# The rows of the transposed tokens at sixteen different offsets modulo 512 bytes

## The chip, the cores and the metric

The kernel runs on one core of a Trainium2 chip. Five engines work side by side on a shared on-chip memory of 128 partitions: TensorE (PE, with its weight loads shown apart as PEld), VectorE (DVE), ScalarE (ACT), GpSimd (POOL) and SyncE (SP), which here only starts transfers. The metric is the device time of one execution in microseconds.

## What is computed

One block of a streaming encoder over 512 tokens of width 1024, in float32. The tokens are normalised and multiplied by one wide matrix, and the ten slices of the result feed two branches, stick-breaking attention with 8 heads and retention with 4 heads, which are gated, projected, merged and added to the input:

```python
h = rms_norm(x, norm_gain)
proj = einsum('bsd,dc->bsc', h, w_in)            # 1024 -> 10 x 1024
(sb_q, sb_k, sb_v, sb_g, r_q, r_k, r_v, r_g, m_sb, m_ret) = split(proj)
out_a = stick_breaking_attention(rms_norm(sb_q), rms_norm(sb_k), sb_v) * silu(sb_g)
out_b = rms_norm(chunkwise_retention(rotary(r_q), rotary(r_k), r_v)) * silu(r_g)
p_a, p_b = out_a @ w_branch_sb, out_b @ w_branch_ret
merged = sigmoid(m_sb + b0) * p_a + sigmoid(m_ret + b1) * p_b
x = x + merged @ w_out
```

## The kernel before

**Split products.** Every float32 operand of a large product is held as two tiles of the matmul's reduced type, a rounded part (`hi`) and the remainder (`lo`). A product is three matmuls, hi by hi, hi by lo and lo by hi (`mm3`, lines 91 to 95; line 86 issues every matmul). In the profile a matmul's row reads `out<-moving,stationary`: the first name behind the arrow is the operand that streams through the array, the second the one that was loaded as weights. Each matmul has a weight load of its own (PEld), which is made while the matmul ahead of it streams.

**The transposed tokens.** `xT_hi` and `xT_lo` (lines 142 and 143) hold the 512 tokens with the model's width on the partitions: 8 rows (`NK`) of 512 numbers, or 2,048 bytes, one row for each 128 of the 1,024 inputs. ACT (line 159) and DVE (line 160) write each row once at the start. Every later group of the input projection reads all 16 rows.

**Groups.** `dense` makes one group: for each of the 8 rows `k`, `load_split` brings 128 by 512 weights, splits them into `hi` and `lo` (lines 115 and 116, or 204 and 205), and for each of 4 blocks `j` one `mm3` adds into a PSUM bank. That is 8 x 4 x 3 = 96 matmuls of 128 x 512. Twenty groups are of the input projection and use `xT`: four each of `qk` and `rqk`, two each of `v`, `sg`, `rv`, `rg`, `ma` and `mb`, in all 1,920 matmuls. In the `qk`, `v` and `rv` groups (argument `rows` true) a 128-column slice of an `xT` row is the stationary operand and the weights stream; in the others the weights are stationary and a whole `xT` row streams. Six more groups (`pa`, `pb`, `fin`) have other tiles in the place of `xT`.

**Side work.** The small matmuls of attention (`z`, `pw`, `po`) and retention (`rz`, `ro`, `rt`) are generators that `Interleaver.step` puts between the matmuls of a group, after every second `j`. TensorE keeps the order of the program.

**Addresses.** The pool `const` lays its tiles one behind another in the order of the code, each rounded up to 32 bytes; the other pools follow. Two tiles have spare room: `vec` (`V_ROOM`) and `m_half` (`M_ROOM`). In the built program `xT_hi` starts at byte 17,888 of each partition and `xT_lo` at 34,272, both 480 modulo 512. A row is 2,048 bytes, so all 16 rows lie at 480. The weight tiles, the tiles of `qk`, `rqk`, `v` and `rv`, the gates, the branch outputs and the temporaries are at 480 as well, and a slice of 128 numbers is 512 bytes, so slices keep it. The one large exception is the pair `wT`, at 128: it streams in `po` and is stationary in `ro`.

Of the kernel before, what the change touches and what calls it, by code (L numbers as in the profile page):

```python
# [7 lines left out]
F32 = mybir.dt.float32  # L8
F32R = mybir.dt.float32r
# [3 lines left out]
P = 128  # L13
S = 512
D = 1024
NT = S // P
NK = D // P
# [9 lines left out]

V_NG, V_BM, V_QG, V_KG, V_RG, V_N = 0, 8, 24, 25, 26, 34

V_ROOM, M_ROOM = 66, 112  # L30


RAW_BUFS = 2
# [34 lines left out]
def hybrid_block(ctx, tc, x, x_t, vecs, w_in, w_a, w_b, w_o, cos_t, sin_t, decay, out):  # L68
# [3 lines left out]
    const = ctx.enter_context(tc.tile_pool(name="const", bufs=1))  # L72
# [66 lines left out]
    nc.scalar.activation(warm, zero, AF.Sigmoid)  # L139

    vec = const.tile([P, V_ROOM], F32, name="vec")[:, :V_N]
    xT_hi = const.tile([P, NK, S], F32R, name="xT_hi")
    xT_lo = const.tile([P, NK, S], F32R, name="xT_lo")

    def first_loads():

# [503 lines left out]
```

## Time and profile before

| | us |
|---|---|
| median of 2 runs | 663.17 |
| lowest, highest | 662.77, 663.58 |
| the profiled execution's own time | 664.18 |
| its span, first to last instruction | 662.4 |
| PE busy in it | 656.3 |
| PEld busy | 546.4 |
| DVE, ACT, POOL busy | 375.9, 260.7, 50.8 |

The span and all rows are of one profiled execution; 1.8 us of its time lie outside the span. Matmuls are pipelined: the start of the next one is earlier than the modelled end of the one before, so the distance of the starts, not the duration, is what a matmul takes from the span.

### The profile page before, as it was taken

What the parts mean: (1) busy time and instruction counts of PE and PEld (TensorE: products, weight loads), DVE (VectorE), ACT (ScalarE), POOL (GpSimd) and SP (SyncE); (2) the same over time, 40 slices, a digit from 0 to 9 for tenths busy, and PEclk for the clock granted to TensorE, in tenths of its full rate; (3) what the DMA queues carried; (4) which work ended last, traced back from release to release, by engine and by line L of the source; (5) the groups of instructions that cost most, each with busy time, mean ns of one, the idle gap of its engine ahead of it and who ended that gap; (6) DMA issues with size and microseconds to landing.
All of it is one profiled execution on the core that took longest, in us unless ns stands there. A gap on an engine that the chain in (4) does not pass through costs nothing.

```text
span 662.4 us, 7979 instructions
## 1 busy us (share of the span) xinstructions
PE 656.3 (99%) x3096; PEld 546.4 (82%) x3096; DVE 375.9 (57%) x560; ACT 260.7 (39%) x416; POOL 50.8 (8%) x50
## 2 busy tenths in 40 slices
PE   8999999999999999999999999999999999999997
PEld 5888888888888888888888888888888888888886
DVE  6456874587497477632334763844862953544632
ACT  4744534464364554422312342433433443422310
POOL 0051000441000400000000001001001001000000
PEclk9999999999999999999999999999999999999999
DMA  8543223322322323233333323222323322335541
GB/s 288 189 128 96 65 63 96 96 64 65 95 64 64 96 63 96 60 99 96 95 96 111 96 64 106 84 80 81 96 70 106 93 66 64 96 95 161 158 159 63
DMA packets 42182, 65.02 MB, mean 98 GB/s; under 512 B 2848, under 2 KB 19488, under 8 KB 42144
## 3 DMA queue, kind: packets, MB, share of 16 engines
q1 hardware_dynamic: 41568, 63.47, 31.2%
q10 hardware_dynamic: 576, 1.05, 0.4%
q8 instruction: 24, 0.39, 0.3%
q14 instruction: 14, 0.11, 0.1%
HBM read 62.41 MB, written 2.10 MB: 97 GB/s over the span
## 4 chain that ended last, share of the span: by engine, by line
PE 99%; DMA 0%; SPq 0%; ACT 0%; DVE 0%; issue 0%; DVEq 0%; ACTq 0%
PE qk_ps L86 14%; PE rqk_ps L86 13%; PE sg_ps L86 7%; PE v_ps L86 7%; PE ma_ps L86 7%; PE rv_ps L86 7%; PE mb_ps L86 7%; PE rg_ps L86 7%; PE fin_ps L86 7%; PE pb_ps L86 7%; PE pa_ps L86 7%; PE po L86 2%; PE z L86 2%; PE rz L86 2%; PE ro L86 2%; PE pw L89 1%
## 5 line engine op out<-in xcount | busy, mean ns | idle before, releaser
L86 PE MATMUL qk_ps<-qk_hi,xT_hi 128*128 128x512 f32 x128 | 51.5, 411 | 0.9 <-ACT xT_hi L159 0.9
L86 PE MATMUL rqk_ps<-xT_hi,rqk_hi 128*128 128x512 f32 x128 | 50.5, 394 | 0.0
L86 PE MATMUL rqk_ps<-xT_hi,rqk_lo 128*128 128x512 f32 x128 | 50.0, 391 | 0.0
L86 PE MATMUL rqk_ps<-xT_lo,rqk_hi 128*128 128x512 f32 x128 | 50.0, 390 | 0.0
L86 PE MATMUL qk_ps<-qk_lo,xT_hi 128*128 128x512 f32 x128 | 49.8, 398 | 0.0
L86 PE MATMUL qk_ps<-qk_hi,xT_lo 128*128 128x512 f32 x128 | 49.5, 395 | 0.0
L86 PE MATMUL pb_ps<-ob,pb_hi 128*128 128x512 f32 x128 | 39.5, 390 | 0.0
L86 PE MATMUL pa_ps<-oa,pa_hi 128*128 128x512 f32 x128 | 39.4, 389 | 0.0
L116 DVE TENSOR_TENSOR rqk_lo<-rqk_raw,rqk_hi 128x1024 fp32r<-128x1024 f32 x16 | 20.8, 1300 | 23.9 <-ACT rqk_hi L115 23.9
L386 DVE TENSOR_TENSOR_SCAN keep<-keep,zero 128x128 f32<-128x128 f32 (+3 forms) x32 | 27.1, 847 | 7.3 <-ACT keep L384 7.3
L86 PEld LDWEIGHTS qk_ps<-qk_hi,xT_hi 128*128 128x128 f32 x128 | 24.5, 192 | 6.2 <-ACT xT_hi L159 1.8
L86 PEld LDWEIGHTS qk_ps<-qk_hi,xT_lo 128*128 128x128 f32 x128 | 24.5, 191 | 5.4
L189 POOL TENSOR_TENSOR rrr<-ms,m_half 128x4 f32<-128x4 f32 x4 | 4.0, 1007 | 316.3 <-DVE ms L188 316.3
L86 PEld LDWEIGHTS qk_ps<-qk_lo,xT_hi 128*128 128x128 f32 x128 | 24.7, 193 | 4.3
L86 PEld LDWEIGHTS rqk_ps<-xT_hi,rqk_lo 128*128 128x128 f32 x128 | 24.1, 188 | 5.0
L86 PEld LDWEIGHTS pb_ps<-ob,pb_hi 128*128 128x128 f32 x128 | 24.0, 188 | 5.0
L86 PEld LDWEIGHTS pa_ps<-oa,pa_hi 128*128 128x128 f32 x128 | 24.0, 188 | 5.0
L86 PEld LDWEIGHTS rqk_ps<-xT_hi,rqk_hi 128*128 128x128 f32 x128 | 24.1, 188 | 4.7
L86 PEld LDWEIGHTS rqk_ps<-xT_lo,rqk_hi 128*128 128x128 f32 x128 | 24.1, 188 | 4.6
L115 ACT CAST rqk_hi<-rqk_raw 128x1024 fp32r<-128x1024 f32 x16 | 16.8, 1050 | 25.8 <-PE rqk_ps L86 16.5
L116 DVE TENSOR_TENSOR qk_lo<-qk_raw,qk_hi 128x1024 fp32r<-128x1024 f32 x14 | 17.6, 1259 | 15.1 <-ACT qk_hi L115 15.1
L86 PE MATMUL v_ps<-v_hi,xT_hi 128*128 128x512 f32 x64 | 26.1, 408 | 0.0
(185 smaller groups left out, 1709.8 us busy)
## 6 DMA issues: line engine op xcount, KB each, us to landing
rqk_raw<-in_w_in SPq DMA_DIRECT2D x32, 256.0 KB, 3.0
qk_raw<-in_w_in SPq DMA_DIRECT2D x28, 256.0 KB, 3.0
v_raw<-in_w_in SPq DMA_DIRECT2D x8, 512.0 KB, 3.9
sg_raw<-in_w_in SPq DMA_DIRECT2D x8, 512.0 KB, 3.6
rv_raw<-in_w_in SPq DMA_DIRECT2D x8, 512.0 KB, 3.6
ma_raw<-in_w_in SPq DMA_DIRECT2D x8, 512.0 KB, 3.6
pa_raw<-in_w_a SPq DMA_DIRECT2D x8, 512.0 KB, 3.9
rg_raw<-in_w_in SPq DMA_DIRECT2D x8, 512.0 KB, 3.6
```

The lines of the kernel that those rows point to most:

```text
L86: tc.keep_in_program_order(nc.tensor.matmul(*a, **k))
L89: tc.keep_in_program_order(nc.tensor.transpose(*a))
L115: nc.scalar.copy(hi, src)
L116: nc.vector.tensor_sub(lo, src, f32(hi))
L189: nc.gpsimd.tensor_tensor(dst, t[:, :width], m_half[:, :width], op=ALU.pow)
L386: nc.vector.tensor_tensor_scan(keep[:, :n][:, ::-1], keep[:, :n][:, ::-1], zero.broadcast_to([P, n]), 1.0, op0=ALU.mult, op1=ALU.add,)
```

## The change

The rows of both tiles get a pitch of 528 numbers (2,112 bytes) in place of 512, of which the first 512 are used, and a tile of 8 numbers (32 bytes) that nothing reads or writes is put between them. `M_ROOM` loses 8 numbers.

```diff
-V_ROOM, M_ROOM = 66, 112
+
+V_ROOM, M_ROOM = 66, 104
+X_PITCH = S + 16
...
-    xT_hi = const.tile([P, NK, S], F32R, name="xT_hi")
-    xT_lo = const.tile([P, NK, S], F32R, name="xT_lo")
+    xT_hi = const.tile([P, NK, X_PITCH], F32R, name="xT_hi")[:, :, :S]
+    const.tile([P, 8], F32, name="between")
+    xT_lo = const.tile([P, NK, X_PITCH], F32R, name="xT_lo")[:, :, :S]
```

In the built program `xT_hi` stays at 17,888 and its row k is at 480 + 64k modulo 512; `xT_lo` starts at 34,816 and its row k is at 64k. So the rows of `xT_hi` take the eight odd multiples of 32 and those of `xT_lo` the eight even ones. `idle`, `ident`, `neg_mask` and `m_half`, which follow, go from 480 to 0. Everything behind `m_half` moves by 1,024 bytes and keeps its offset modulo 512. No instruction is added, taken away or moved on any engine, and every access has the shape that it had.

## Rows read from the trace of the kernel before

**Rows 1.** The page's head, PE's busy time, and its granted clock in 40 slices.
```profile
span 662.4 us, 7979 instructions
PE 656.3 (99%) x3096; PEld 546.4 (82%) x3096; DVE 375.9 (57%) x560; ACT 260.7 (39%) x416; POOL 50.8 (8%) x50
...
PEclk9999999999999999999999999999999999999999
```
**Rows 2.** The chain that ended last, by engine.
```profile
PE 99%; DMA 0%; SPq 0%; ACT 0%; DVE 0%; issue 0%; DVEq 0%; ACTq 0%
```
**Rows 3.** Tile xT_hi on PE: count, duration min/median/max in ns, first and last start.
```profile
L86 PE MATMUL rqk_ps<-xT_hi,rqk_hi x128: 388/390/477, 341.2 to 518.5; 128*128 128x512 f32 x128
L86 PE MATMUL rqk_ps<-xT_hi,rqk_lo x128: 388/390/398, 341.6 to 518.9; 128*128 128x512 f32 x128
L86 PE MATMUL v_ps<-v_hi,xT_hi x64: 387/390/481, 29.6 to 163.6; 128*128 128x512 f32 x64
L86 PE MATMUL v_ps<-v_lo,xT_hi x64: 386/390/397, 29.8 to 163.8; 128*128 128x512 f32 x64
```
**Rows 4.** Groups by form, 12 to 663 us: busy us, mean ns of one, idle before.
```profile
L86 PE MATMUL rqk_ps<-xT_hi,rqk_lo 128*128 128x512 f32 x128 | 50.0, 391 | 0.0
L86 PE MATMUL rqk_ps<-xT_lo,rqk_hi 128*128 128x512 f32 x128 | 50.0, 390 | 0.0
...
L86 PE MATMUL qk_ps<-qk_hi,xT_lo 128*128 128x512 f32 x124 | 48.1, 392 | 0.0
...
L86 PE MATMUL v_ps<-v_hi,xT_lo 128*128 128x512 f32 x64 | 25.1, 393 | 0.0
...
L86 PE MATMUL pa_ps<-oa,pa_lo 128*128 128x512 f32 x64 | 24.9, 390 | 0.0
...
L86 PE MATMUL fin_ps<-fin_lo,mg_hi 128*128 128x512 f32 x64 | 24.9, 389 | 0.0
```
**Rows 5.** Timeline of PE, a settled stretch: start us, duration us, line, operation.
```profile
299.71 0.39 PE L86 MATMUL ma_ps<-xT_hi,ma_hi 128*128 128x512 f32 x1
...
305.83 0.39 PE L86 MATMUL ma_ps<-xT_hi,ma_hi 128*128 128x512 f32 x1
```
**Rows 6.** Timeline of PE, behind a block of attention scores.
```profile
77.83 0.34 PE L86 MATMUL z<-qk_hi,qk_lo 128*128 128x384 f32 x1
78.01 0.40 PE L86 MATMUL sg_ps<-xT_hi,sg_hi 128*128 128x512 f32 x1
...
80.33 0.39 PE L86 MATMUL sg_ps<-xT_lo,sg_hi 128*128 128x512 f32 x1
```
**Rows 7.** Timeline of PE, retention scores, both operands at 480.
```profile
386.67 0.28 PE L86 MATMUL rz<-rqk_lo,rqk_hi 128*128 128x256 f32 x1
...
387.27 0.40 PE L86 MATMUL rg_ps<-xT_hi,rg_hi 128*128 128x512 f32 x1
```
**Rows 8.** Timeline of PE, retention outputs, moving at 480, stationary at 128.
```profile
396.58 0.28 PE L86 MATMUL ro<-rv_hi,wT 128*128 128x256 f32 x1
...
399.10 0.40 PE L86 MATMUL rqk_ps<-xT_hi,rqk_hi 128*128 128x512 f32 x1
```
**Rows 9.** Groups by form, one matmul each: at 396.53, 386.50 and 82.32 us.
```profile
L86 PE MATMUL rqk_ps<-xT_hi,rqk_lo 128*128 128x512 f32 x1 | 0.4, 398 | 0.0
...
L86 PE MATMUL rg_ps<-xT_hi,rg_lo 128*128 128x512 f32 x1 | 0.4, 390 | 0.0
...
L86 PE MATMUL po<-wT,v_hi 128*128 128x512 f32 x1 | 0.4, 398 | 0.0
```
**Rows 10.** Tile ident on PE: transposes, columns as in rows 3.
```profile
L89 PE MATMUL pw<-ident,beta x80: 270/272/273, 65.3 to 271.0; 128*128 128x128 f32 x80
...
L89 PE MATMUL pqk<-ident,qraw x64: 269/272/273, 41.8 to 238.1; 128*128 128x128 f32 x64
...
L89 PE MATMUL rt<-ident,roraw x32: 269/272/273, 408.7 to 567.0; 128*128 128x128 f32 x32
```
**Rows 11.** The page's costliest group, with PE's wait for the first row.
```profile
L86 PE MATMUL qk_ps<-qk_hi,xT_hi 128*128 128x512 f32 x128 | 51.5, 411 | 0.9 <-ACT xT_hi L159 0.9
```

## The prediction

> **What bounds the kernel now.** I read the page first. TensorE is busy for 656.3 of 662.4 us, and the chain that ended last is 99% PE [rows 1, 2]. So a gain or loss on PE goes to the end nearly in full, and one on DVE or ACT does not, unless PE begins to wait for it. [...]
>
> The second view is the spacing of the matmuls, since the only thing that this change can alter is how fast PE reads. A settled stretch of the `ma` group has 27 matmuls between the starts at 299.71 and 305.83 us: 6.12 us / 27 = 226.7 ns each [rows 5]. The duration of one is 390 ns there; the difference, 163 ns, is pipeline, so a duration of 390 ns stands for a spacing of 226.7 and one of 398 ns for about 235. The median of every large group is 390 [rows 3], and the groups that don't touch `xT` (`pa`, `fin`) have means of 389 and 390 [rows 4]. For 256 columns, five `rz` matmuls take 387.27 - 386.67 = 0.60 us, 120 ns each [rows 7]. Two sizes give a line: (226.7 - 120) / 256 = 0.417 ns for a column, and 226.7 - 512 x 0.417 = 13.3 ns for each matmul besides. [...] For 1,920 matmuls the 13.3 ns are 25.5 us, 3.8% of the time.
>
> What comes on top is little. The matmuls that carry no trailing transposes (hi by lo and lo by hi) have group means of 390 to 393 [rows 4], those left out there between these: weighted by their counts about 1 ns over 390, which for 1,920 is 2 us. The hi-by-hi groups have maxima near 480 [rows 3], but that is the time of the transposes put in ahead of them, 272 ns long and overlapped [rows 10], which no address of `xT` touches.
>
> **The change part by part.** *The writing of `xT`.* The rows are still written 2,048 bytes at a time, once. PE's wait for the first is 0.9 us [rows 11]; I take no change, and 0.9 us either way bounds it.
>
> *`ident` and `idle` go from 480 to 0.* `idle` feeds eight matmuls on data that nobody uses, ahead of the first real one. `ident` streams in 80 + 64 + 32 = 176 transposes [rows 10]. If a differing offset costs 8 ns each (priced below), that is 1.4 us; the other end is 1.4 us gained. I take nothing.
>
> *The offsets of the rows.* This is the whole question. Three measurements bear on it, each from `wT`, which is at 128 where its partner is at 480, a difference of 160 bytes modulo 512.
>
> First, a constant difference costs nothing: 21 `ro` matmuls take 399.10 - 396.58 = 2.52 us, 120.0 ns each [rows 8], the same as `rz` with no difference [rows 7]. That also says that the 13.3 ns is not a collision of equal offsets: it is paid in full at another one.
>
> Secondly, a change of the difference from one matmul to the next does cost. The last `rqk` matmul ahead of that `ro` block streams `xT_hi` while the first weights from `wT` are loaded, and lasts 398 ns; the last `rg` matmul ahead of an `rz` block, where sizes change too but offsets don't, lasts 390 [rows 9]. The first `po` matmuls, 512 columns wide like the `qk` matmuls ahead of them, last 398 at 82.32 us [rows 9]. So a switch is 8 ns on that matmul.
>
> Thirdly, PE takes some ten matmuls to settle after a disturbance. Behind a block of `z` (384 columns, same offsets) the ten `xT` matmuls from 78.01 to 80.33 us take 2.32 us, 232 ns each, 5.3 ns over the settled spacing [rows 6].
>
> [...]
>
> After the change the difference between the moving and the stationary offset switches all the time. In a product of three the `xT` tiles come as hi, lo, hi (weights stationary) or hi, hi, lo (weights moving), so two of three steps change it by 32 bytes, and every twelfth matmul by 64 more as `k` goes on. I can't see a 32-byte switch in the trace; its ends are 0 (the constant difference of rows 8) and 8 ns (the 160-byte switch of rows 9). I take the 5.3 ns of rows 6, an average over many states of a disturbed pipeline, for the matmuls behind a switch: 1,920 x 2/3 x 5.3 ns = 6.8 us. The 2 us of unsettled spacing that exist now go up in it, so the sum is **+4.8 us**. At the lower end it is -2 us (all settles), at the upper 1,920 x 8 ns - 2 = +13.4 us.
>
> Against the profiled execution's own 664.2 us that is 669.0. It lies 1.0 us above the median of the runs, 663.2, so I forecast 668.0 as a median.
>
> **The rivals.** *A: offsets don't matter.* For it: rows 7 and 8, 120 ns at both differences; also that 32 bytes is a small step, 8 columns or 3.3 ns of streaming, which PE may absorb. Against it: rows 9. Then the time stays where it is, 663 us, with 2 us less at most.
>
> *B: faster.* The 13.3 ns would be due to weight loads that meet the stream in the same part of the memory, as both start at the same offset, and spreading the rows would avoid the meeting. For it: the charge is the same for each matmul and each has one weight load. Against it: `ro` pays it in full at a difference of 160 [rows 8]. All of it gone would be 663.2 - 25.5 = 637.7 us, half of it 650. [...]
>
> *C: slower by more than 2%.* Each switch costs what the 160-byte one does, and the return costs too, so that every `xT` matmul lasts 398 ns or more, with none settled. For it: 398 is what two of the three single matmuls of rows 9 show, at their switch. Against it: the switch here is a fifth as large, and one of three steps has none. From 1,920 x 8 - 2 = 13.4 us on, it gives 676.6 us or more; the point from which it decides is a mean duration of 398 ns in the `xT` groups. An error upward of this size is the most that the trace of before has shown for one matmul.
>
> **How the numbers follow.** Forecast (some of the switches cost, 665 to 672 us): 0.46. A (661 to 664): 0.32. B (below 655): 0.10. C (from 676 on): 0.12. A range that leaves out B and the upper part of C runs from **661 to 677 us**; about 0.82 lies in it. Two per cent, 13.3 us, is about what a measurement of this kernel can tell from no change. Faster by more: B, 0.10. Slower by more: most of C, 0.11. Within: forecast, A and the rest of C, 0.79.
>
> **What would show it.** In the profile after, the medians of the `xT` groups should be above 390 ns (392 to 396), while those of `pa`, `pb` and `fin` stay at 389 or 390, and the stretch at 299.7 to 305.8 us should no longer be even. If A is right, the medians stay at 390. If B is right, they fall below 386 in the `xT` groups alone. If C is right, the means are at 398 or over. `ro` and `po`, whose operands keep their offsets, should show no change in any case. The clock should read 9 in every slice; ACT and DVE should have the same busy times. I would be wrong if the cost of a difference depends on its size in a way that 160 bytes doesn't show, since that is the only difference that the trace of before contains.

## The result, and the profile after

The changed kernel takes 670.98 us (median of 2 runs, 670.91 to 671.06) against 663.17: a ratio of 1.0118, 95% interval [1.0074, 1.0161]. It is slower by 7.8 us, inside the forecast range and 3 us above the forecast of 668.0. The profiled execution takes 671.06 us, 6.9 more than that of before.

The page of after, its head, busy times, granted clock and the chain by engine, beside [rows 1, 2]:

```profile
span 669.3 us, 7979 instructions
PE 663.0 (99%) x3096; PEld 544.2 (81%) x3096; DVE 375.3 (56%) x560; ACT 260.8 (39%) x416; POOL 51.0 (8%) x50
PEclk9999999999999999999999999999999999999999
PE 93%; DMA 2%; DVE 1%; POOL 1%; ACT 1%; issue 1%; SPq 0%; DVEq 0%; POOLq 0%
```

PE is busy 6.7 us longer; DVE, ACT and POOL work as long as before to within 0.6 us, and the granted clock reads 9 in all 40 slices of both. The chain now takes a turn through POOL and a transfer early in the kernel, which is one wait of 0.2 us for a tile of attention (`pqk` for `qraw`) and not where the time went.

The groups of after by form, from 12 us on (busy us, mean ns of one, idle before), beside [rows 4, 8]:

```profile
L88 PE MATMUL rqk_ps<-xT_hi,rqk_hi 128*128 128x512 f32 x128 | 51.0, 399 | 0.0
L88 PE MATMUL rqk_ps<-xT_lo,rqk_hi 128*128 128x512 f32 x128 | 50.6, 396 | 0.0
L88 PE MATMUL rqk_ps<-xT_hi,rqk_lo 128*128 128x512 f32 x128 | 50.3, 393 | 0.0
...
L88 PE MATMUL v_ps<-v_hi,xT_lo 128*128 128x512 f32 x64 | 25.2, 394 | 0.0
...
L88 PE MATMUL pa_ps<-oa,pa_lo 128*128 128x512 f32 x64 | 24.9, 389 | 0.0
...
L88 PE MATMUL fin_ps<-fin_lo,mg_hi 128*128 128x512 f32 x64 | 24.9, 389 | 0.0
L88 PE MATMUL ro<-rv_hi,wT 128*128 128x256 f32 x80 | 15.6, 281 | 0.0
```

The two `rqk` groups without transposes went from 390 and 391 to 396 and 393; `pa` and `fin`, which don't read `xT`, stand at 389. In all 24 kinds of `xT` matmul the mean rose, by 1 to 6 ns. Counts times rises add up to 6.7 us. Durations have modelled ends, so the starts are the better measure: summed over the trace from the first `v` matmul on, the distances from each `xT` matmul to the next start rise from 421.4 to 429.2 us, by 7.8, and those of all other matmuls together by 0.3. So nearly the whole loss is in the spacing of the `xT` matmuls.

The medians say that it is most matmuls and not a few. Tile `xT_hi` on PE (count, duration min/median/max in ns, first and last start), beside [rows 3]:

```profile
L88 PE MATMUL rqk_ps<-xT_hi,rqk_hi x128: 387/395/483, 344.2 to 524.5; 128*128 128x512 f32 x128
L88 PE MATMUL rqk_ps<-xT_hi,rqk_lo x128: 387/393/400, 344.7 to 525.0; 128*128 128x512 f32 x128
L88 PE MATMUL v_ps<-v_hi,xT_hi x64: 387/394/483, 28.3 to 164.9; 128*128 128x512 f32 x64
L88 PE MATMUL v_ps<-v_lo,xT_hi x64: 389/396/499, 28.7 to 165.1; 128*128 128x512 f32 x64
```

Every median of this tile was 390 and is 393 to 396; the minimum hardly moved. And the stretch of `ma` that was even, beside [rows 5], in the timeline (start us, duration us), 26 matmuls apart:

```profile
300.35 0.40 PE L88 MATMUL ma_ps<-xT_lo,ma_hi 128*128 128x512 f32 x1
...
306.40 0.40 PE L88 MATMUL ma_ps<-xT_hi,ma_hi 128*128 128x512 f32 x1
```

6.05 us / 26 = 232.7 ns each, where it was 226.7. That is the 232 ns of the unsettled stretch in [rows 6], now all the time.

The first `v` matmul starts at 28.3 us here and at 29.6 in [rows 3]. What follows it takes 669.3 - 28.3 = 641.0 us against 632.8, 8.2 us more; the start of this execution was 1.3 us shorter, which the change did not cause (last section).

### The profile page after: what moved, and what is told of

It is laid out like the page before. It is cut to its first block, busy times and chain, and to the rows that moved or that the text cites. A ratio compares the mean times of both kernels' runs of the same rounds, so it can differ in the third digit from the quotient of the medians.

```text
span 669.3 us, 7979 instructions
## 1 busy us (share of the span) xinstructions
PE 663.0 (99%) x3096; PEld 544.2 (81%) x3096; DVE 375.3 (56%) x560; ACT 260.8 (39%) x416; POOL 51.0 (8%) x50
## 4 chain that ended last, share of the span: by engine, by line
PE 93%; DMA 2%; DVE 1%; POOL 1%; ACT 1%; issue 1%; SPq 0%; DVEq 0%; POOLq 0%
PE rqk_ps L88 13%; PE qk_ps L88 10%; PE rv_ps L88 7%; PE ma_ps L88 7%; PE mb_ps L88 7%; PE sg_ps L88 7%; PE rg_ps L88 7%; PE pa_ps L88 7%; PE pb_ps L88 7%; PE fin_ps L88 7%; PE v_ps L88 5%; PE po L88 2%; PE z L88 2%; PE rz L88 2%; PE ro L88 2%; PE pw L91 1%
## 5 line engine op out<-in xcount | busy, mean ns | idle before, releaser
L88 PE MATMUL sg_ps<-xT_hi,sg_hi 128*128 128x512 f32 x64 | 25.9, 405 | 0.0
```

Source lines behind the costliest of these rows:

```text
L88: tc.keep_in_program_order(nc.tensor.matmul(*a, **k))
```

## The experiments

Eleven kernels ran, each the kernel before with other offsets for some tiles, never with another order of instructions. "Constant" means that all 16 rows of `xT` have the same offset. Unless a line says otherwise, tiles of unused room keep every other tile at its offset of before. The ratio is one of means, so it can differ a little from that of the medians beside it.

| run | what differs from the kernel before | median us | before beside it | ratio, 95% interval |
|---|---|---|---|---|
| e1_const32 | all rows 32 bytes on | 672.12 | 664.13 | 1.0129 [1.011, 1.0148] |
| e2_hilo32 | `xT_lo` alone 32 on | 671.46 | 664.13 | 1.0106 [1.0084, 1.0127] |
| e3_pitch64 | row k of both tiles 64k on | 668.18 | 664.13 | 1.0067 [1.0049, 1.0085] |
| e4_hilo128 | `xT_lo` alone 128 on | 669.80 | 664.13 | 1.0089 [1.0074, 1.0104] |
| e5_const256 | all rows 256 on | 664.47 | 664.39 | 1.0004 [0.9993, 1.0016] |
| e6_hilo256 | `xT_lo` alone 256 on | 664.19 | 664.39 | 0.9992 [0.9982, 1.0003] |
| e7_all_at_0 | everything but `wT` 32 on | 663.85 | 664.39 | 0.9998 [0.9987, 1.0009] |
| e8_const160 | all rows 160 on | 673.84 | 664.39 | 1.0154 [1.0134, 1.0174] |
| e9_ident_at_0 | `ident` and its neighbours alone at 0 | 663.34 | 663.99 | 0.9992 [0.998, 1.0005] |
| e10_const64 | all rows 64 on | 668.59 | 663.99 | 1.0079 [1.0063, 1.0095] |
| e11_wT480 | `wT` at 480 like all others | 663.71 | 663.99 | 1.0 [0.999, 1.001] |

The theory at the start was the prediction's: a *switch* of the difference between the moving and the stationary offset costs, a constant difference doesn't. Rival 1: an unequal offset costs by itself. Rival 2: the rise comes from `ident`, `idle` and the masks, which the change moves too.

### A constant difference of 32 bytes

```diff
+    const.tile([P, 8], F32, name="ahead")
     xT_hi = const.tile([P, NK, S], F32R, name="xT_hi")
     xT_lo = const.tile([P, NK, S], F32R, name="xT_lo")
+    const.tile([P, 120], F32, name="behind")
```

> All 16 rows at offset 0 modulo 512, pitch 2,048 as before: every xT row differs from its partner by the same 32 bytes, and nothing else moves its offset. Theory (a switch of the difference from matmul to matmul costs, a constant one does not): no change, 663 us within 1.5, medians of the xT groups 390 ns. Rival 1 (an unequal offset costs by itself): all 1,920 matmuls pay the 5 to 6 ns seen after the change, 671 to 674 us, medians 394 to 396. Rival 2 (the rise came from ident, idle and the masks, which are back at 480 here): no change, as the theory.

Measured 1.0129. Nothing switches here within a group, and it is as slow as the change. Tile `xT_hi` on PE, and two starts 18 matmuls apart in `mb`:

```profile
L86 PE MATMUL rqk_ps<-xT_hi,rqk_lo x128: 389/396/401, 344.4 to 525.5; 128*128 128x512 f32 x128
...
L86 PE MATMUL v_ps<-v_lo,xT_hi x64: 389/396/403, 28.7 to 164.6; 128*128 128x512 f32 x64
```
```profile
550.66 0.40 PE L86 MATMUL mb_ps<-xT_hi,mb_hi 128*128 128x512 f32 x1
...
554.86 0.40 PE L86 MATMUL mb_ps<-xT_hi,mb_hi 128*128 128x512 f32 x1
```

4.20 us / 18 = 233.3 ns, steadily. The prediction's theory is refuted, and so is rival 2, since `ident` is at 480 here. Nor is it a collision with the other computing engines, whose tiles now lie 32 bytes off `xT` as well: settled matmuls around which DVE, ACT and POOL are all idle are 233.2 ns apart here and 226.7 in the kernel before. ("Settled" means that at least a dozen matmuls of 512 columns came since one of another width; these figures are read from the starts in the traces.)

### `xT_lo` alone moved by 32 and by 128 bytes

```diff
     xT_hi = const.tile([P, NK, S], F32R, name="xT_hi")
+    const.tile([P, 8], F32, name="between")
     xT_lo = const.tile([P, NK, S], F32R, name="xT_lo")
+    const.tile([P, 120], F32, name="behind")
```

(For 128: 32 numbers between, 96 behind.)

> All rows of xT_hi at 480, all of xT_lo at 0 (32 bytes on), pitch 2,048; ident and the rest at 480. Two of three steps switch the difference by 32 bytes, none by the row. Theory: most of the rise is there, 668 to 671 us, medians of the xT groups 392 to 396. Rival 1: only the third of the matmuls that reads xT_lo pays, 665 to 666. Rival 2 (ident): 663.

> As e2_hilo32, but xT_lo lies 128 bytes on (at 96). Theory in its plain form (a larger switch costs as much or more): 669 to 673 us. A second form of it: the settled spacings 120 and 226.7 ns are 9 and 17 times 13.3 ns, which is the streaming time of 32 columns or 128 bytes, so the phase may repeat after 128 bytes; then a switch by 128 is none and the time is 663 us. Rival 1: a third of the matmuls pays, 665 to 666.

Measured 1.0106 and 1.0089. Two thirds of the matmuls have equal offsets in these kernels, but much more than a third of the loss is there, so rival 1 in the form "each unequal matmul pays for itself" doesn't fit either. Tile `xT_hi` of the first:

```profile
L86 PE MATMUL rqk_ps<-xT_hi,rqk_hi x128: 389/393/478, 345.2 to 525.3; 128*128 128x512 f32 x128
L86 PE MATMUL rqk_ps<-xT_hi,rqk_lo x128: 387/392/398, 345.7 to 525.8; 128*128 128x512 f32 x128
...
L86 PE MATMUL v_ps<-v_lo,xT_hi x64: 389/397/400, 30.7 to 166.3; 128*128 128x512 f32 x64
```

All of these read `xT_hi`, at the offset of the weights, and none has a median of 390. In `rqk` the loads beside these two streams are of equal offset as well, and yet they stand at 393 and 392: one unequal matmul in three keeps its neighbours from settling. In `v` the matmul with 397 is the one beside whose stream `xT_lo` is loaded, while the next, whose own weights are `xT_lo`, is not slow (tile `xT_lo`):

```profile
L86 PE MATMUL v_ps<-v_hi,xT_lo x64: 389/389/401, 30.9 to 166.5; 128*128 128x512 f32 x64
```

### The pitch alone

```diff
-    xT_hi = const.tile([P, NK, S], F32R, name="xT_hi")
-    xT_lo = const.tile([P, NK, S], F32R, name="xT_lo")
+    xT_hi = const.tile([P, NK, S + 16], F32R, name="xT_hi")[:, :, :S]
+    xT_lo = const.tile([P, NK, S + 16], F32R, name="xT_lo")[:, :, :S]
```

> Pitch 2,112 bytes, row k of both tiles at 480 + 64k: hi and lo have the same offset, and the difference switches by 64 bytes only at each new row, every twelfth matmul. Theory: about 160 switches; at 8 ns for the switch alone 664.5 us, and if each starts ten unsettled matmuls (53 ns), 160 x 53 ns = 8.5 us less the 2 to 3 that are there now, about 669. Rival 1: seven of eight rows are unequal, 670 us. The two are told apart inside a row: by the theory the last matmuls of the twelve are back at 390, by rival 1 all twelve are above it but in row 0.

Measured 1.0067. This kernel holds eight differences in one run, each for twelve matmuls. Starts in an `mb` group, in stretches without side work: the last half of row 0 (six matmuls), all of row 3, where the moving operand is 192 bytes on (twelve), and the last half of row 4, 256 bytes on (six):

```profile
523.21 0.39 PE L86 MATMUL mb_ps<-xT_hi,mb_hi 128*128 128x512 f32 x1
...
524.57 0.40 PE L86 MATMUL mb_ps<-xT_hi,mb_hi 128*128 128x512 f32 x1
...
530.12 0.39 PE L86 MATMUL mb_ps<-xT_hi,mb_hi 128*128 128x512 f32 x1
...
532.92 0.39 PE L86 MATMUL mb_ps<-xT_hi,mb_hi 128*128 128x512 f32 x1
...
535.66 0.39 PE L86 MATMUL mb_ps<-xT_hi,mb_hi 128*128 128x512 f32 x1
...
537.02 0.40 PE L86 MATMUL mb_ps<-xT_hi,mb_hi 128*128 128x512 f32 x1
```

1.36 / 6 = 226.7, 2.80 / 12 = 233.3 and again 1.36 / 6 = 226.7 ns. Over all groups in which `xT` streams, the settled matmuls in the second halves of rows 0 to 7 are 226.7, 228.9, 233.1, 233.3 and then 226.7, 228.8, 233.1, 233.3 ns apart: the four values repeat after four rows, or 256 bytes. That gave the new theory: what counts is the difference of the two offsets modulo 256 bytes.

### A difference of 256, constant and switching

```diff
+    const.tile([P, 64], F32, name="ahead")
     xT_hi = const.tile([P, NK, S], F32R, name="xT_hi")
     xT_lo = const.tile([P, NK, S], F32R, name="xT_lo")
+    const.tile([P, 64], F32, name="behind")
```

(For the switching one the 64 numbers stand between the two tiles.)

> All 16 rows 256 bytes on (at 224 modulo 512), everything else as before. Rival 1 in its plain form (any unequal offset costs): 671 to 674 us, like the run with a constant 32. New theory, from the rows of the run with pitch 2,112, where rows 0 and 4 settle at 227 ns and the others at 229 to 234: what a matmul takes depends on the difference of the two offsets modulo 256, and at 256 it is as good as none: 663 us, xT medians 390.

> xT_hi at 480, xT_lo 256 bytes on, so two of three steps switch the difference by 256 bytes, the largest there is modulo 512. The prediction's theory (a switch costs): 668 us or more. New theory (only the difference modulo 256 counts): no switch at all, 663 us, medians 390.

Measured 1.0004 and 0.9992: no difference. Tile `xT_hi`, first of the constant, then of the switching kernel:

```profile
L86 PE MATMUL rqk_ps<-xT_hi,rqk_lo x128: 389/389/398, 341.3 to 518.6; 128*128 128x512 f32 x128
L86 PE MATMUL v_ps<-v_hi,xT_hi x64: 387/390/478, 28.8 to 163.2; 128*128 128x512 f32 x64
```
```profile
L86 PE MATMUL rqk_ps<-xT_hi,rqk_lo x128: 388/389/398, 342.1 to 519.4; 128*128 128x512 f32 x128
L86 PE MATMUL v_ps<-v_hi,xT_hi x64: 387/390/478, 30.0 to 164.0; 128*128 128x512 f32 x64
```

In the second kernel two of three steps switch by the largest amount that there is modulo 512, for nothing. So it is neither the switch nor the inequality.

### Equal offsets elsewhere

```diff
+    const.tile([P, 8], F32, name="ahead")
     xT_hi = const.tile([P, NK, S], F32R, name="xT_hi")
     xT_lo = const.tile([P, NK, S], F32R, name="xT_lo")
```

> Everything behind xT is 32 bytes on as well, so xT, the weights and all other tiles are at 0 modulo 512 and equal again; only wT stays where it was and is 128 off. New theory (the difference counts): 663 to 664 us, xT medians 390. Rival 3 (offset 0, or a multiple of 64, is the bad place, which would also explain the run with all xT rows at 0): 670 us or more.

Measured 0.9998, medians as before:

```profile
L86 PE MATMUL rqk_ps<-xT_hi,rqk_lo x128: 387/389/398, 340.4 to 517.8; 128*128 128x512 f32 x128
```

The rows of `xT` are at 0 here as in the first experiment, which was slow. What differs is the partner. Here the offset itself didn't matter (0.9998 at 0 with the partner at 0), the difference did (1.0129 at 0 with the partner at 480).

### The difference that `ro` has

```diff
+    const.tile([P, 40], F32, name="ahead")
     xT_hi = const.tile([P, NK, S], F32R, name="xT_hi")
     xT_lo = const.tile([P, NK, S], F32R, name="xT_lo")
+    const.tile([P, 88], F32, name="behind")
```

> All 16 rows 160 bytes on, at 128 like wT: the very difference at which the ro block of the kernel before takes 120 ns for 256 columns, and from which the prediction concluded that a constant difference costs nothing. If that reading carries over to 512 columns: 663 us, medians 390. If every difference that is no multiple of 256 costs at 512 columns: 668 to 674, medians 392 to 397, with ro itself unchanged at 120 ns.

Measured 1.0154, the highest ratio of all, though its interval overlaps that of the constant 32. Starts of the same kernel: 21 `ro` matmuls, 29 of `mb`, and 45 of `qk`:

```profile
400.55 0.28 PE L86 MATMUL ro<-rv_hi,wT 128*128 128x256 f32 x1
...
403.05 0.40 PE L86 MATMUL rqk_ps<-xT_hi,rqk_hi 128*128 128x512 f32 x1
```
```profile
529.75 0.39 PE L86 MATMUL mb_ps<-xT_hi,mb_lo 128*128 128x512 f32 x1
...
536.54 0.40 PE L86 MATMUL mb_ps<-xT_lo,mb_hi 128*128 128x512 f32 x1
```
```profile
10.96 0.39 PE L86 MATMUL qk_ps<-qk_hi,xT_hi 128*128 128x512 f32 x1
...
21.45 0.40 PE L86 MATMUL qk_ps<-qk_hi,xT_hi 128*128 128x512 f32 x1
```

`ro`: 2.50 us / 21 = 119 ns, as in [rows 8]. `mb`, at the same distance of 160 bytes: 6.79 us / 29 = 234.1 ns. But the two have opposite signs: in `mb` the moving operand is at 128 and the stationary one at 480, in `ro` it is the other way round, which modulo 256 is a difference of 96 and not 160. The groups with `ro`'s sign are those with `xT` stationary. There `qk` takes 10.49 us / 45 = 233.1 ns. So the very same difference is free in `ro`, at 256 columns, and costs 6.4 ns over the 226.7 in `qk`, at 512.

### `ident`, the sign, and `wT`

The other part of the change alone, and two smaller questions:

```diff
-V_ROOM, M_ROOM = 66, 112
+V_ROOM, M_ROOM = 66, 104
...
     xT_lo = const.tile([P, NK, S], F32R, name="xT_lo")
+    const.tile([P, 8], F32, name="behind")
```

> The kernel before with only the other part of the change: idle, ident, neg_mask and m_half at 0, all xT rows at 480. Theory (the xT offsets make the rise): 663 to 664 us, at most the 1.4 us that was given as the bound for the 176 transposes. Rival 2 (ident and the masks): 668 or more.

Measured 0.9992: nothing, and the transposes last as long as in [rows 10]:

```profile
L89 PE MATMUL pw<-ident,beta x80: 270/272/276, 64.3 to 270.0; 128*128 128x128 f32 x80
```

All rows 64 bytes on:

```diff
+    const.tile([P, 16], F32, name="ahead")
     xT_hi = const.tile([P, NK, S], F32R, name="xT_hi")
     xT_lo = const.tile([P, NK, S], F32R, name="xT_lo")
+    const.tile([P, 112], F32, name="behind")
```

> All rows 64 bytes on. In the run with pitch 2,112 the rows with +64 for the moving operand were at 229 ns and those with -64 at 233, so the sign counts: groups with xT moving should sit near 229 (durations 391 to 392), groups with xT stationary near 233 (395 to 396): 1,152 x 2.5 ns + 768 x 6.5 ns less the 3 us of unsettled spacing of before = 5 us, 668 us. If the sign is an artefact of rows that had not settled: both alike, 231 on average, 668 too, and the medians tell it.

Measured 1.0079, 668.59 us. Groups by form (mean ns); in `rqk` the moving operand is 64 ahead of the weights, in `v` it is 64 behind:

```profile
L86 PE MATMUL rqk_ps<-xT_hi,rqk_lo 128*128 128x512 f32 x128 | 50.3, 393 | 0.0
L86 PE MATMUL rqk_ps<-xT_lo,rqk_hi 128*128 128x512 f32 x128 | 49.9, 390 | 0.0
...
L86 PE MATMUL v_ps<-v_lo,xT_hi 128*128 128x512 f32 x64 | 25.3, 395 | 0.0
L86 PE MATMUL v_ps<-v_hi,xT_lo 128*128 128x512 f32 x64 | 25.3, 395 | 0.0
```

The sign counts, as the pitch run had it, at this distance: 390 and 393 against 395. It is the sign and not the role: in the pitch run the groups with `xT` stationary, settled as above, take 226.5, 233.0, 232.2, 230.0 and 226.6, 233.1, 232.3, 229.7 ns in rows 0 to 7, so there rows 3 and 7 are the cheaper ones, whose difference of -192 is 64 modulo 256. At 32 the sign doesn't count (396 in both kinds of group in the first experiment).

`wT` brought to 480:

```diff
+    const.tile([P, 88], F32, name="ahead")
     wT_pair = [const.tile([P, NT, S], F32R, name=f"wT_{q}") for q in range(2)]
+    const.tile([P, 40], F32, name="behind")
```

> The kernel before with wT moved to 480, so that every operand of every large matmul has the same offset. Theory: the disturbances at the entries and exits of po and ro go: 8 x (9 + 26) ns at ro and about 24 x 5 ns in po, 0.4 us in all, 0.06%, which the times can hardly show but the rows can: the last matmul ahead of ro at 390 ns, po at 390. If equality does not matter there: 398 as before.

Measured 1.0, as 0.4 us can't be seen. The last matmul ahead of a `ro` block, by form in a window of 50 ns at 397.22 us (the second line is the matmul ahead of it):

```profile
L86 PE MATMUL rqk_ps<-xT_hi,rqk_lo 128*128 128x512 f32 x1 | 0.4, 390 | 0.0
L86 PE MATMUL rqk_ps<-xT_lo,rqk_hi 128*128 128x512 f32 x1 | 0.4, 389 | 0.0
```

390 where [rows 9] had 398. The traces have eight such entries: 398 at all of them in the kernel before, 388 to 390 here; the first `po` matmul of each block goes from 396 to 399 down to 388 to 390. So the 398 was the price of streaming from one offset while the next weights come from another. It is in the load that goes on beside the stream, not in a matmul's own weights, which are at 480 in both kernels. In the run with `xT_lo` 128 on, the matmul behind pays as well (`v_lo,xT_hi` 396, `v_hi,xT_lo` 397), so how the price is shared out is not settled.

## Why the prediction was right, and where its working was not

The time came out inside the range, but by luck: the mechanism that the sum was made of is refuted.

**The bound and the place.** Right: the loss is on PE, in the `xT` groups, and none of it is hidden. The medians rose to 393 to 396 (forecast 392 to 396), `pa` and `fin` stayed, `ro` stayed, the clock and the other engines stayed.

**The edits at nothing.** Right: `ident` and its neighbours cost nothing (0.9992).

**"A constant difference costs nothing."** This step failed. It was read from `ro`, at 256 columns, and carried over to 512, where the same difference takes 233.1 ns against 226.7 (the kernel with it has a ratio of 1.0154). The trace of before held no settled stretch of 512 columns at an unequal offset; the `po` matmul of [rows 9], at 398, was a single one of that kind and was read as a switch.

**"A change of the difference does cost."** It fell with it. A switch by 256 is free (0.9992) and a constant 32 is as dear as the change (1.0129). What the 398 of [rows 9] priced was the difference itself.

**The sum, +4.8 us.** The price per matmul was near: 5.3 ns of unsettled spacing was taken, and the spacing in the even stretch rose by 6.0. That is luck, since the 5.3 ns was the settling behind a block of other width at equal offsets, and no run ties the two together. The factor of two thirds was wrong, since it came from the count of switches. Of the 1,920 matmuls, 1,600 have operands that differ modulo 256; the other 320 (rows 0 and 4 of `xT_hi`) each have one of these next to them. Without that factor the sum is 1,920 x 5.3 ns - 2 us = 8.2 us, 671.4 us as a median, and 670.98 was measured.

**The rivals.** A, that offsets don't matter, is out: the same load beside the same stream takes 226.7 or 233.3 ns by their addresses. B is out as well: no arrangement of the twelve profiled beside before brought a settled spacing clearly under 226.7; the lowest is 226.5, in row 0 of the pitch run. C, a mean of 398, was not reached: the `xT` groups without transposes are at 393 to 397. Two per cent is not the limit of what can be told here either: the intervals reach 0.1 to 0.4% to each side.

**What stays open.** What it is that repeats every 256 bytes, and why the `ro` matmuls, of 256 columns, don't pay (119 ns at a difference of 96). No run here tells. All differences were multiples of 32 bytes, and each of the eight modulo 256 occurs in some run, once the sign is counted; smaller steps were not tried.

## What to carry to other kernels

Where PE is the bound and every matmul of 512 float32 columns has a weight load of its own, try giving the streamed and the stationary tiles the same offset modulo 256 bytes. This is one kernel; here other differences cost 0.7 to 1.5% of the kernel, and a tile of 32 unused bytes, or a padded row pitch, is enough to lose it. Spreading the rows over sixteen offsets to avoid conflicts did the reverse (1.0118). And a cost that is read at one size of an instruction is not proven for another: a difference that was free at 256 columns cost 6.4 ns a matmul at 512.

## What the runs showed that was not expected

The settled spacing takes few values. By the moving offset less the stationary one, modulo 256, they are 226.7 ns at 0, 228.8 to 230 at 64, 232 to 233.4 at 32, 96, 128, 192 and 224, and 234.2 at 160. Here 32 and 224 are the two kinds of group of the constant 32, 160 and 96 those of the constant 160, and 64, 128 and 192 come from the pitch run and the constant 64. Equal offsets and the common 233.3 lie 13.3 and 20 ns above 512 columns at the 0.417 ns of the prediction's line.

One unequal matmul in three costs almost as much as three (1.0106 against 1.0129).

The start differs between executions by more than many effects. PE's timeline, first of before, then of after:

```profile
7.52 1.91 PE L86 MATMUL qk_ps<-qk_lo,xT_hi 128*128 128x512 f32 x4
9.23 1.46 PE L86 MATMUL qk_ps<-qk_hi,xT_lo 128*128 128x512 f32 x4
```
```profile
6.43 1.09 PE L88 MATMUL qk_ps<-qk_lo,xT_hi 128*128 128x512 f32 x4
7.36 1.08 PE L88 MATMUL qk_ps<-qk_hi,xT_lo 128*128 128x512 f32 x4
```

Four matmuls take 1.71 us in the one, 427 ns each, and 0.93 us in the other, 233 ns each; the runs with equal offsets modulo 256 show both kinds of start (the longest `qk_lo,xT_hi` matmul lasts 629 ns before and in the run with `xT_lo` 256 on, 397 ns in the run with all rows 256 on). A view of this stretch of before prints a full granted clock, but the trace's record of the clock begins only at 10.0 us there, just when the spacing falls to 227 ns, so it says nothing of what came earlier. In the run with `xT_lo` 32 on the record covers such a stretch (first the timeline, then the window's length, busy time of PE, PEld, DVE, ACT and POOL, granted clock, DMA share and GB/s):

```profile
7.64 1.91 PE L86 MATMUL qk_ps<-qk_lo,xT_hi 128*128 128x512 f32 x4
9.34 1.71 PE L86 MATMUL qk_ps<-qk_hi,xT_lo 128*128 128x512 f32 x4
```
```profile
7.30:10.60 3.30, 3.30 (x9) 2.54 (x8) 3.27 (x7) 1.91 (x3) 0.00 (x0) 0.50 1.04 377
```

1.70 us / 4 = 425 ns, at a granted clock of 0.50. So the author's estimate is that the slow start of before, at 427 ns, was a clock of 0.50 too, though it is not recorded there. It is most of the 1.3 us by which the first `v` matmul was earlier after the change, and a reason to compare stretches and not spans.
